# A hybrid encoder on one core: v of branch B ahead of the heads, silu gates of branch A behind pairs of heads, and sums of weights taken by VectorE

## The chip, the cores and the metric

The kernel runs on one core of a Trainium2 chip. The metric is the device time of one execution in microseconds, as the median of several runs; lower is better. Engines are named as in the profile: PE (TensorE, matmul), PEld (its weight loads), DVE (VectorE), ACT (ScalarE), POOL (GpSimd), SP (SyncE), and a q behind a name means the engine's own queue of DMA issues and waits.

## The reference

Two residual layers over 512 positions of width 1024. Each layer normalises its input, projects it once, and feeds three branches, whose gated outputs are merged and projected again.

```python
for l in range(DEPTH):
    h = rms_norm(x, norm_gain[l])
    proj = jnp.einsum('bld,dn->bln', h, w_in[l])
    (qa, fa_f, fa_b, ia, za, ub, vb, zb, qc, kc, vc, zc, g_a, g_b, g_c) = jnp.split(proj, split_at, axis=-1)
    ya = hgrn2_bidirectional(qa, fa_f, fa_b, ia, lower[l]).astype(x.dtype)
    ya = rms_norm(ya, hg_norm_gain[l]).reshape(B, L, HG_W) * jax.nn.silu(za)
    yb = spatial_gating(jax.nn.gelu(ub), jax.nn.gelu(vb), sg_ln_gain[l], sg_ln_bias[l],
                        w_spatial[l], b_spatial[l]) * jax.nn.silu(zb)
    ...
    yc = window_attention(qh, kh, vh, sink_logits[l]) * jax.nn.silu(zc)
    merged = (jax.nn.sigmoid(g_a) * jnp.einsum('blw,wd->bld', ya, w_branch_a[l])
              + jax.nn.sigmoid(g_b) * jnp.einsum('blw,wd->bld', yb, w_branch_b[l])
              + jax.nn.sigmoid(g_c) * jnp.einsum('blw,wd->bld', yc, w_branch_c[l]))
    x = x + jnp.einsum('bld,de->ble', merged, w_out[l])

def spatial_gating(u, v, ln_g, ln_b, w_s, b_s):
    vn = layer_norm(v, ln_g, ln_b).reshape(B, L // SG_CHUNK, SG_CHUNK, SG_GROUPS, SG_GW)
    mixed = jnp.einsum('gts,bnsgc->bntgc', w_s, vn) + b_s.T[None, None, :, :, None]
    return u * mixed.reshape(B, L, SG_W)
```

Branch A is a gated recurrence with four heads, run in both directions. Branch B mixes positions within chunks of 128 by a weight per group (w_s); v goes through a layer norm first. Branch C is attention in a window with eight query heads. The shift ln_b of the layer norm meets w_s in the mixing, so its part of the result is ln_b times the sum of each row of w_s: the kernel adds that to the bias b_s ahead of time.

## The kernel before, in words

Everything is float32. A product of activations and weights is done as three fast matmuls: both operands are split into a high part (a rounded copy by ACT, L267: wh of a weight) and a low part (a subtraction by DVE, L268: wl), and high x high, low x high and high x low are added up in PSUM (L470, L505, L517, L1172). The weights come in tiles of 128 x 1024 in the order of a list, weight_plan(). SP loads them (L239) in that order, some ahead of their use, and every tile is split once. Matmuls of plain float32 (the attention's values L831, the recurrence's L926 to L1029, the spatial mixing L1072, and the two products L1058) lie between them.

The weights of a layer come in this order: queries of branch C, its z gates and keys, the values of branch A (C_IA), then for each of the four heads of branch A the query, two forget gates and the z gate (C_QA, C_FF, C_FB, C_ZA), then v of branch B (C_VB), then the merge. Beside the blocks of weight matmuls run "sides": generators that do a piece of other work each time the main program calls advance(us). Such a generator yields the time that it has used, or None to wait for another turn. The attention is one side, begun before the heads; the gated recurrence of a pair of heads (gla) is added after each odd head; ln_v, which prepares the layer norm of v and the corrected bias, is added after v was projected; spatial mixing comes later. LAG and QLAG are numbers of turns that the attention lets pass between sending data through DRAM to transpose it and using it.

The build puts each engine's instructions into an order of its own, by when their inputs are ready; each engine then works in its order and stops at an instruction whose inputs are late. DMAs issued by SP or POOL stand in those engines' orders too.

Steps touched here, with lines of the profile: do_vb (L1045, gelu of v: ACT L1038 and L1040, DVE L1039 and L1041); ln_v (statistics L1053 and L1054, rstd L324 to L331, a matmul of ones with the weights ws L1058 whose result is each sum on all partitions, L1061 which adds the shift to the bias tile br, L1066 which normalises v); the z gates (L1095 and L1096); rope_row and rope_tables of the next layer (SP L336, SP L343, DVE L344), issued after head 1's block; the attention's scores (PE L781 and L782), their masked maxima (DVE L783), exponentials (ACT L795), scaling (DVE L806), transposes (DVE L813) and the way through DRAM (POOL L817, L818); and w_conv_to (L257), which adds two weights for a faster form of some products, the last of each layer on POOL.

Of the kernel before, what the change touches and what calls it, by code (L numbers as in the profile page):

```python
# [14 lines left out]
F32 = mybir.dt.float32  # L15
# [37 lines left out]
def weight_plan():  # L53

    plan = []

    def quarters(kind):

        for r, u in ((0, 0), (1, 0), (1, 1), (0, 1)):
            for i in range(2):  # L60
                plan.append(kind + (u, 2 * r + i))

    def nat(c):
        for i in range(4):
            plan.append(("n", c, i))

    nat(C_QC)
    for g in range(2):
        plan.append(("z", g))
    for i in range(2):  # L70
        plan.append(("k", C_KV, i))
    for g in range(2, 4):
        plan.append(("z", g))
    nat(C_IA)
    for h in range(H):
        for c in (C_QA, C_FF, C_FB, C_ZA):
            plan.append(("t", c + P * h))
    nat(C_VB)
    def merge(blocks):
        for n, j in enumerate(blocks):  # L80
            plan.append(("t", C_GC + P * j))
            if n % 2 == 0:
                plan.append(("b", 2, j, blocks[n + 1]))

    merge(MERGE[:6])

    quarters(("g", C_UB))
    for br, cg in ((0, C_GA), (1, C_GB)):
        quarters(("g", cg))
        for j in GATED:  # L90
            plan.append(("b", br, j, j + 1))
    merge(MERGE[6:])
    quarters(("o",))
    return plan
# [77 lines left out]
    return bass.AP(a.tensor, a.offset + off, [list(a.ap[0])] + [list(d) for d in dims])  # L172


def hybrid_kernel(tc, x, wpk, brow, gainb, pvec, wsp, trig, amask, imask, out):
    nc = tc.nc
    from contextlib import ExitStack

    with ExitStack() as es:
        cp = es.enter_context(tc.tile_pool(name="const", bufs=1))  # L180
        wp = es.enter_context(tc.tile_pool(name="wts", bufs=4))
        sb = es.enter_context(tc.tile_pool(name="work", bufs=2))
        pp = es.enter_context(tc.tile_pool(name="psum", bufs=3, space=PSUM))
        dp = es.enter_context(tc.tile_pool(name="spill", bufs=1, space=bass.MemoryType.DRAM))
        build(nc, tc, cp, wp, sb, pp, dp, x, wpk, brow, gainb, pvec, wsp, trig, amask, imask, out)


LAG, QLAG = 6, 9
N_M4, N_T2, N_PM, N_PS = 19, 7, 3, 5


def build(nc, tc, cp, wp, sb, pp, dp, x, wpk, brow, gainb, pvec, wsp, trig, amask, imask, out):
    V, S, G, E = nc.vector, nc.scalar, nc.gpsimd, nc.tensor


# [12 lines left out]
    def small(n):  # L208
        return sb.tile([P, n], F32, name=nm("sm"), tag="small", bufs=24)
# [4 lines left out]
    def ps_side(shape=(P, 512), dt=F32):  # L214
        return pp.tile(list(shape), dt, name=nm("ps"), tag="ps", bufs=N_PS)
# [29 lines left out]
    def raw(k):  # L245
        if k not in raws:
            w_load_to(k + 1)
        return raws[k]

    def w_conv_to(i, order=free, eng=V):  # L250
        while wstate["conv"] < min(i, len(OPERANDS)):
            n = wstate["conv"]
            k, add, form, _ = OPERANDS[n]
            r = raw(k)
            if form:
                raws[form[0]] = hold["t"][:, 2] if form[0][2] == 0 else m4()
                (G if form[0][1] % NW == NW - 8 else V).tensor_tensor(raws[form[0]], r, raw(form[1]), ALU.add)  # L257
            hi = wp.tile([P, 1024], F32R, name=nm("wh"), tag="wh", bufs=N_HI)
            lo = wp.tile([P, 1024], F32R, name=nm("wl"), tag="wl", bufs=N_LO)
            split(r, hi, lo, order, eng)  # L260
            if add is not None:
                G.dma_start(r, wpk[add], accum_op=ALU.add)
            his[n], los[n] = hi, lo
            wstate["conv"] += 1
# [326 lines left out]
    for l in range(L):  # L591
# [454 lines left out]
            gelu(po, vg[tb // 2][:, tb % 2, :])  # L1046

        def ln_v():
            mv = small(8)
            mv2 = mv.rearrange("p (n c) -> p n c", c=2)  # L1050
            for n in range(NT):
                st = small(6)
                V.bn_stats(st, vg[n // 2][:, n % 2, :])  # L1053
                V.bn_aggr(mv2[:, n, :], st)  # L1054
            r = rstd(mv2[:, :, 1], NT, 1.0)

            po = ps_side((P, 4, P))
            E.matmul(po, ones, ws, start=True, stop=True)  # L1058
            for g in range(4):
                b = br[:, g * P : (g + 1) * P]  # L1060
                V.scalar_tensor_tensor(b, po[:, g, :], lnb[:, g : g + 1], b, ALU.mult, ALU.add)  # L1061
            yield 2.5
            yield None
            for n in range(NT):
                v = vg[n // 2][:, n % 2, :]
                V.tensor_scalar(v, v, mv2[:, n, 0:1], r[:, n : n + 1], ALU.subtract, ALU.mult)  # L1066
                yield 0.7

        def spatial(g):
            po = ps_side((P, 4, P))  # L1070
# [6 lines left out]
            V.tensor_tensor(u, u, y.rearrange("p n t -> p (n t)"), ALU.mult)  # L1077
            yield 2.0


        glas = []
        lnv, spat = ln_v(), [spatial(g) for g in range(4)]
        for h in range(H):
            po = main_t()
            q = t2()
            S.copy(q, po)
            advance(2.6)
            ff, kd = m4((P, 2, T)), m4((P, 2, T))
            for d in range(2):
                po = main_t()  # L1090
                gates(po, d, h, ff, kd)
                advance(2.6)
            po = main_t()
            z = yA[h // 2][:, h % 2, :]
            S.activation(z, po, AF.Sigmoid)  # L1095
            V.scalar_tensor_tensor(z, po, hg[:, h : h + 1], z, ALU.mult, ALU.mult)  # L1096
            glas.append(gla(h, q, ff, kd, z))
            if h % 2 == 1:
                sides.append(together(glas[-2:]))
            advance(4.0)  # L1100
            if h == 1 and more:
                rr = rope_row(l + 1)
                tabs[0] = rope_tables(rr)
        nat_units(do_vb, 2.6)
        sides.append(lnv)

# [354 lines left out]
def host_arrays(inputs):  # L1463
    a = {k: np.asarray(v) for k, v in inputs.items()}
    ct = np.ascontiguousarray
    f = a["x"].dtype
    arrays = {}
    arrays["x"] = ct(a["x"].reshape(T, D))
    arrays["wpk"] = pack_weights(a["w_in"], a["w_branch_a"], a["w_branch_b"], a["w_branch_c"], a["w_out"])

    def swap(g):
        return np.concatenate([g[:, 32:], g[:, :32]], axis=1)

    qg, kg = a["q_norm_gain"], a["k_norm_gain"]
    arrays["brow"] = ct(
        np.concatenate(
            [
                a["b_spatial"].reshape(L, 512),
                qg,
                swap(qg),  # L1480
                kg,
                swap(kg),
                a["sink_logits"],
            ],
            axis=1,
        )
    )
    arrays["gainb"] = ct(a["norm_gain"])
    lbl = a["lb_logits"].reshape(L, 8, P).transpose(2, 0, 1).reshape(P, 16)
    hgt = a["hg_norm_gain"].transpose(2, 0, 1).reshape(P, 8)  # L1490
    lnt = [a[n].reshape(L, 4, P).transpose(2, 0, 1).reshape(P, 8) for n in ("sg_ln_gain", "sg_ln_bias")]
    arrays["pvec"] = ct(np.concatenate([lbl, hgt] + lnt, axis=1))
    arrays["wsp"] = ct(a["w_spatial"].transpose(0, 3, 1, 2))

    half = 32
    inv = (10000.0 ** (-np.arange(half, dtype=np.float64) / half)).astype(np.float32)
    ang = np.arange(T, dtype=np.float32)[:, None] * inv[None, :]
    c = np.cos(ang.astype(np.float64)).astype(np.float32)
    s = np.sin(ang.astype(np.float64)).astype(np.float32)
    cc = np.concatenate([c, c], axis=1).reshape(NT, P, 64).transpose(1, 0, 2)  # L1500
    sn = np.concatenate([-s, s], axis=1).reshape(NT, P, 64).transpose(1, 0, 2)
    arrays["trig"] = ct(np.stack([cc, sn], axis=1))
    qi, ki = np.arange(P)[:, None], np.arange(P)[None, :]
    arrays["amask"] = ct(
        np.concatenate(
            [np.where(ki >= qi, 0.0, MASKED), np.zeros((P, P)), np.where(ki <= qi, 0.0, MASKED)], axis=1
        ).astype(np.float32)
    )
    si, ti = (np.arange(P) % 32)[:, None], np.arange(32)[None, :]
    xr = si ^ ti  # L1510
    masks = [(xr >= m) & (xr < 2 * m) for m in (1, 2, 4, 8)]
    masks += [(xr < 16) & (np.arange(P)[:, None] // 32 == b) for b in range(4)]
    arrays["imask"] = ct(np.stack(masks, axis=1).astype(np.int32))
    assert arrays["x"].dtype == f
    return arrays


NAMES = ["x", "wpk", "brow", "gainb", "pvec", "wsp", "trig", "amask", "imask"]


# [16 lines left out]
```

## Time and profile before

| what | us |
|---|---|
| median of 3 runs | 1067.1 (1066.8 to 1068.72) |
| the profiled execution | 1067.53 |
| its span in the profile | 1065.8 |
| what lies around the span | 1.7 |
| granted TensorE clock | 1.00 |

In the profile, a row of instructions gives the engine, the line, the operation, the output tile and its inputs (in_ is a tensor in DRAM), how many there were and how long they took. Idle time before an instruction stands in brackets with what ended it. The rows of orders under the change hold no times: they are the instructions of one engine in the order in which it works through them.

### The profile page before, as it was taken

What the parts mean: (1) busy time and instruction counts of PE and PEld (TensorE: products, weight loads), DVE (VectorE), ACT (ScalarE), POOL (GpSimd) and SP (SyncE); (2) the same over time, 40 slices, a digit from 0 to 9 for tenths busy, and PEclk for the clock granted to TensorE, in tenths of its full rate; (3) what the DMA queues carried; (4) which work ended last, traced back from release to release, by engine and by line L of the source; (5) the groups of instructions that cost most, each with busy time, mean ns of one, the idle gap of its engine ahead of it and who ended that gap; (6) DMA issues with size and microseconds to landing.
All of it is one profiled execution on the core that took longest, in us unless ns stands there. A gap on an engine that the chain in (4) does not pass through costs nothing.

```text
span 1065.8 us, 19216 instructions
## 1 busy us (share of the span) xinstructions
PE 1054.4 (99%) x7720; PEld 904.8 (85%) x7720; DVE 822.4 (77%) x1525; ACT 536.1 (50%) x817; POOL 125.7 (12%) x178
## 2 busy tenths in 40 slices
PE   9999999999999999999999999999999999999998
PEld 8888777687889998988778887778778999999886
DVE  6885687779988776578897666887897877765885
ACT  5355865544336543545444367665433564445442
POOL 0220110100001110111102201100100011111020
PEclk9999999999999999999999999999999999999999
DMA  8663353932336865783947444543524378557755
GB/s 313 189 208 97 131 183 115 313 92 85 104 86 166 207 193 162 171 251 111 301 150 234 143 141 165 209 139 103 141 96 138 82 201 223 148 141 204 229 159 137
DMA packets 53768, 177.49 MB, mean 167 GB/s; under 512 B 6192, under 2 KB 10800, under 8 KB 53680
## 3 DMA queue, kind: packets, MB, share of 16 engines
q1 hardware_dynamic: 28656, 100.25, 28.1%
q0 software_dynamic: 23296, 71.84, 26.9%
q10 hardware_dynamic: 1728, 4.20, 1.0%
q8 instruction: 60, 0.98, 0.4%
q14 instruction: 28, 0.23, 0.1%
HBM read 154.23 MB, written 22.02 MB: 165 GB/s over the span
## 4 chain that ended last, share of the span: by engine, by line
PE 89%; DVE 6%; DMA 2%; ACT 1%; issue 1%; POOL 0%; SPq 0%; POOLq 0%; ACTq 0%; DVEq 0%
PE pm L517 39%; PE pm L1172 13%; PE ps L1172 13%; PE pm L470 11%; PE pm L505 2%; DMA wr<-in_wpk 2%; PE ps L831 2%; PE ps L926 1%; PE ps L1000 1%; DVE wl L268 1%; PE ps L781 1%; PE ps L782 1%; PE ps L317 1%; PE ps L1072 1%; PE ps L1011 1%
## 5 line engine op out<-in xcount | busy, mean ns | idle before, releaser
L267 ACT CAST wh<-wr 128x1024 fp32r<-128x1024 f32 x172 | 178.6, 1050 | 200.3 <-PE pm L517 113.4
L268 DVE TENSOR_TENSOR wl<-wr,wh 128x1024 fp32r<-128x1024 f32 x172 | 212.3, 1245 | 61.0 <-issue 22.5
L517 PE MATMUL pm<-hth,wh 128*128 128x512 f32 x448 | 177.1, 395 | 0.4 <-ACT wh L267 0.4
L517 PE MATMUL pm<-hth,wl 128*128 128x512 f32 x448 | 175.1, 391 | 0.3 <-DVE wl L268 0.3
L517 PE MATMUL pm<-htl,wh 128*128 128x512 f32 x448 | 175.1, 391 | 0.0
L517 PEld LDWEIGHTS pm<-hth,wh 128*128 128x128 f32 x448 | 84.1, 188 | 19.7 <-ACT wh L267 1.3
L517 PEld LDWEIGHTS pm<-hth,wl 128*128 128x128 f32 x448 | 84.1, 188 | 19.6 <-DVE wl L268 1.2
L517 PEld LDWEIGHTS pm<-htl,wh 128*128 128x128 f32 x448 | 84.2, 188 | 16.5
L517 PE MATMUL pm<-m,wh 128*128 128x512 f32 x256 | 90.9, 395 | 0.0
L470 PE MATMUL pm<-wh,hth 128*128 128x512 f32 x192 | 74.6, 398 | 0.7 <-ACT hth L267 0.5
L470 PE MATMUL pm<-wh,htl 128*128 128x512 f32 x192 | 73.6, 393 | 0.2 <-DVE htl L268 0.2
L470 PE MATMUL pm<-wl,hth 128*128 128x512 f32 x192 | 73.6, 393 | 0.0
L972 DVE TENSOR_TENSOR m<-m,f 128x512 f32<-128x512 f32 x96 | 62.8, 686 | 5.0 <-PE ps L957 3.3
L517 PEld LDWEIGHTS pm<-m,wh 128*128 128x128 f32 x256 | 47.5, 188 | 9.7 <-issue 0.5
L1172 PE MATMUL ps<-hth,wl 128*128 128x256 f32 x192 | 54.5, 284 | 0.6 <-DVE wl L268 0.6
L1172 PE MATMUL ps<-hth,wh 128*128 128x256 f32 x192 | 54.6, 284 | 0.0
L1172 PE MATMUL pm<-hth,wl 128*128 128x256 f32 x192 | 54.4, 283 | 0.0
L1172 PE MATMUL pm<-htl,wh 128*128 128x256 f32 x192 | 54.3, 283 | 0.0
L1172 PE MATMUL ps<-htl,wh 128*128 128x256 f32 x192 | 54.3, 283 | 0.0
L1172 PE MATMUL pm<-hth,wh 128*128 128x256 f32 x192 | 54.3, 283 | 0.0
L1172 PE MATMUL pm<-m,wh 128*128 128x256 f32 x288 | 52.8, 284 | 0.5 <-ACT m L1252 0.5
L268 DVE TENSOR_TENSOR wl<-hold,wh 128x1024 fp32r<-128x1024 f32 x32 | 39.1, 1222 | 18.0 <-PE pm L1172 17.2
(269 smaller groups left out, 2477.3 us busy)
## 6 DMA issues: line engine op xcount, KB each, us to landing
wr<-in_wpk SPq DMA_DIRECT2D x172, 512.0 KB, 4.5
hold<-in_wpk POOLq DMA_DIRECT2D x40, 512.0 KB, 5.6
pd<-m POOLq DMA_DIRECT2D x20, 512.0 KB, 3.5
m<-pd POOLq DMA_DIRECT2D x20, 512.0 KB, 5.5
wr<-in_wpk POOLq DMA_DIRECT2D x16, 512.0 KB, 6.0
m<-in_x SPq DMA_DIRECT2D x8, 512.0 KB, 7.5
m<-xd POOLq DMA_DIRECT2D x16, 256.0 KB, 7.0
m<-in_wpk POOLq DMA_DIRECT2D x8, 512.0 KB, 6.8
```

Source lines behind the costliest of these rows:

```text
L267: order(S.copy(hi_dst, src))
L268: order(eng.tensor_tensor(lo_dst, src, hi_dst.bitcast(F32), ALU.subtract))
L317: E.matmul(warm[:, :P], ident, ident, start=True, stop=True)
L470: E.matmul(po, a, b[:, o : o + 512], start=first and n == 0, stop=last and n == len(passes) - 1)
L505: E.matmul(po[:, k, :], a, b[:, o : o + 256], start=n == 0, stop=n == 23)
L517: E.matmul(po, s, m, start=n == 0, stop=n == 3 * nk - 1)
L781: E.matmul(sp[:, :nk], qt[qb][:, h, :], ktt[0][:, g, k0 * P : k1 * P], start=True, stop=False)
L782: E.matmul(sp[:, :nk], qt[qb][:, h, :], ktt[1][:, g, k0 * P : k1 * P], start=False, stop=True)
L831: E.matmul(po[64 * g : 64 * g + 64], vC[:, k0 + kb, 64 * g : 64 * g + 64], pt[:, :, 128 * g : 128 * g + 128], start=kb == 0, stop=kb == le ...
L926: E.matmul(cb[p0 : p0 + 32, slot, j // 4, :], kk(32 * j), qq(32 * j), start=True, stop=True, tile_position=(0, p0),)
L972: V.tensor_tensor(v, v, custom(ff, of, ([sd, 2], [2, ng], [0, m])), ALU.mult)
L1172: E.matmul(banks[g][:, r, :], a, b, start=not onto and (r, kt, n) == (0, 0, 0), stop=kt == 3 and n == 2, skip_group_check=onto is not None ...
```

## The change

The change has four parts.

- weight_plan: v of branch B (C_VB) comes ahead of the heads, and each pair of heads is followed by its two z gates (C_ZA) instead of each head by its own. The program follows: do_vb and ln_v's start come ahead of the loop over heads, and do_za(h), a new function with the old lines of the z gate, is called twice after each pair, behind the gated recurrence's start.
- ln_v: the matmul with ones goes. SP loads the transposed weights wsr (a new input, the same numbers in the order group, t, s), VectorE sums over s into ss (128 x 4), POOL stores these 512 numbers into DRAM and reads them back to all partitions into the same tile wsum, and the four steps that add to br read wsum from SBUF.
- LAG and QLAG go from 6 and 9 to 8 and 11.
- w_conv_to: all sums of two weights are VectorE's; before, POOL did the two adds of the last product of each layer.

```diff
@@ weight_plan
     nat(C_IA)
+    nat(C_VB)
     for h in range(H):
-        for c in (C_QA, C_FF, C_FB, C_ZA):
+        for c in (C_QA, C_FF, C_FB):
             plan.append(("t", c + P * h))
-    nat(C_VB)
+        if h % 2 == 1:
+            for g in (h - 1, h):
+                plan.append(("t", C_ZA + P * g))
...
-LAG, QLAG = 6, 9
+LAG, QLAG = 8, 11
...
-                (G if form[0][1] % NW == NW - 8 else V).tensor_tensor(raws[form[0]], r, raw(form[1]), ALU.add)
+                V.tensor_tensor(raws[form[0]], r, raw(form[1]), ALU.add)
...
         def ln_v():
+
+            wsum = t2((P, 4, P))
+            nc.sync.dma_start(wsum, wsr[l])
+            for _ in range(3):
+                yield None
+            ss = small(4)
+            V.tensor_reduce(ss, wsum, AX, ALU.add)
+            sd = dp.tile([4, P], F32, name=nm("sd"))
+            G.dma_start(sd.rearrange("g t -> t g"), ss)
+            G.dma_start(wsum.rearrange("p g t -> p (g t)"), sd.rearrange("g t -> (g t)").partition_broadcast(P))
+            yield 0.5
...
             r = rstd(mv2[:, :, 1], NT, 1.0)
-
-            po = ps_side((P, 4, P))
-            E.matmul(po, ones, ws, start=True, stop=True)
-            for g in range(4):
-                b = br[:, g * P : (g + 1) * P]
-                V.scalar_tensor_tensor(b, po[:, g, :], lnb[:, g : g + 1], b, ALU.mult, ALU.add)
             yield 2.5
             yield None
             for n in range(NT):
                 v = vg[n // 2][:, n % 2, :]
                 V.tensor_scalar(v, v, mv2[:, n, 0:1], r[:, n : n + 1], ALU.subtract, ALU.mult)
                 yield 0.7
+
+            for g in range(4):
+                b = br[:, g * P : (g + 1) * P]
+                V.scalar_tensor_tensor(b, wsum[:, g, :], lnb[:, g : g + 1], b, ALU.mult, ALU.add)
+            yield 0.5
...
+        def do_za(h):
+            po = main_t()
+            z = yA[h // 2][:, h % 2, :]
+            S.activation(z, po, AF.Sigmoid)
+            V.scalar_tensor_tensor(z, po, hg[:, h : h + 1], z, ALU.mult, ALU.mult)
+            advance(4.0)
...
         lnv, spat = ln_v(), [spatial(g) for g in range(4)]
+        nat_units(do_vb, 2.6)
+        sides.append(lnv)
         for h in range(H):
...
-            po = main_t()
-            z = yA[h // 2][:, h % 2, :]
-            S.activation(z, po, AF.Sigmoid)
-            V.scalar_tensor_tensor(z, po, hg[:, h : h + 1], z, ALU.mult, ALU.mult)
-            glas.append(gla(h, q, ff, kd, z))
+            glas.append(gla(h, q, ff, kd, yA[h // 2][:, h % 2, :]))
             if h % 2 == 1:
                 sides.append(together(glas[-2:]))
-            advance(4.0)
+                for g in (h - 1, h):
+                    do_za(g)
             if h == 1 and more:
                 rr = rope_row(l + 1)
                 tabs[0] = rope_tables(rr)
-        nat_units(do_vb, 2.6)
-        sides.append(lnv)
```

What this does to the orders is shown at three places of layer 0. Line numbers of the changed kernel are higher by 3 up to L1045 and by more behind that: L783, L806, L813 and L268 become L786, L809, L816 and L271; L1053 and L1061 become L1067 and L1079.

First SP's order around the load of rr, the rows of the next layer's rotary factors. Before (L239 loads a weight, L343 the tables):

```order
L239 DMA wr_1360<-in_wpk 128x1024
L239 DMA wr_1427<-in_wpk 128x1024
L239 DMA wr_1475<-in_wpk 128x1024
L336 DMA rr_1502<-in_brow 128x264
L343 DMA tabs_1504<-in_trig 128x512 x2
L239 DMA wr_1621<-in_wpk 128x1024
L239 DMA wr_1716<-in_wpk 128x1024
L239 DMA wr_1773<-in_wpk 128x1024
```

Of the change, the same place (L242 loads a weight, L339 rr):

```order
L242 DMA wr_1601<-in_wpk 128x1024
L242 DMA wr_1699<-in_wpk 128x1024
L242 DMA wr_1828<-in_wpk 128x1024
L339 DMA rr_1886<-in_brow 128x264
L346 DMA tabs_1888<-in_trig 128x512 x2
L242 DMA wr_1925<-in_wpk 128x1024
L242 DMA wr_2011<-in_wpk 128x1024
```

So rr's load stands five instructions later in SP's order: behind four more weights and the load of wsum, which is new (L1054, 13 weight loads ahead of rr). In VectorE's order the last read of the old rr (L794) stands ahead of the splits of wr_1601, wr_1699 and wr_1828; before, it stood behind the split of wr_1475, the last weight ahead of rr.

Second VectorE's order in the second block of the attention, from the scaling of its scores on. Before (wl_1424 is the low part of a weight; block 2's scores follow block 1's transposes):

```order
L806 TENSOR_SCALAR scores_1131<-scores_1131,sm_1126 128x3x128 x8
L1096 SCALAR_TENSOR_TENSOR m_187_1038<-pm_1213,pvc,m_187_1038 128x512
L813 STREAM_TRANSPOSE m_225_1254<-scores_1131 128x8x4x32
L813 STREAM_TRANSPOSE m_228_1272<-scores_1131 128x8x4x32
L813 STREAM_TRANSPOSE m_234_1297<-scores_1131 128x8x4x32
L844 TENSOR_TENSOR m_86_466<-ps_1317,m_86_466 128x2x128
L783 ISA scores_1327,sm_1324<-ps_1328,am,rows_574 128x3x128
```

Of the change (t_228 is wsum, br the bias tile; the rows behind these are one step of rstd between every two L786, eight L786 in all, and then the split of the first head's forget gate weight, L271 wl_1503):

```order
L816 STREAM_TRANSPOSE m_230_1293<-scores_1164 128x8x4x32
L816 STREAM_TRANSPOSE m_235_1313<-scores_1164 128x8x4x32
L1068 BN_AGGR sm_1350<-sm_1351 128x2
L1067 BN_STATS sm_1354<-m_196_1070 128x6
L1067 BN_STATS sm_1357<-m_203_1154 128x6
L816 STREAM_TRANSPOSE m_242_1345<-scores_1164 128x8x4x32
L1068 BN_AGGR sm_1350<-sm_1354 128x2
L1068 BN_AGGR sm_1350<-sm_1357 128x2
L1067 BN_STATS sm_1360<-m_203_1154 128x6
L1079 SCALAR_TENSOR_TENSOR br_1010<-t_228_1277,pvc,br_1010 128x128
L1068 BN_AGGR sm_1350<-sm_1360 128x2
L1079 SCALAR_TENSOR_TENSOR br_1010<-t_228_1277,pvc,br_1010 128x128
```

The statistics of v and the steps on br now lie between the transposes of one block and the scores of the next; the reduction (L1058) lies ahead of the eight scalings (L809).

Third TensorE's order at the first weights that follow (ps_1446 is the sixth of block 2's eight scores; there are five such places in PSUM, so it takes that of the first). Before, the ones matmul lay behind the heads:

```order
L517 MATMUL pm_2874<-hth_127,wh_2840 128x512
L517 MATMUL pm_2874<-htl_128,wh_2840 128x512
L517 MATMUL pm_2874<-hth_127,wl_2841 128x512
L1058 MATMUL ps_2973<-ws_1042,ones 128x512
L517 MATMUL pm_2979<-m_443_2670,wh_2939 128x512
```

Of the change, it is gone from there, and at the attention TensorE takes the high parts of three weights ahead before it needs wl_1503:

```order
L520 MATMUL pm_1465<-hth_127,wl_1433 128x512
L520 MATMUL pm_1522<-hth_127,wh_1502 128x512
L784 MATMUL ps_1446<-m_161_932,m_148_834 128x384
L785 MATMUL ps_1446<-m_162_933,m_148_834 128x384
L520 MATMUL pm_1522<-htl_128,wh_1502 128x512
L784 MATMUL ps_1450<-m_161_932,m_148_834 128x384
L785 MATMUL ps_1450<-m_162_933,m_148_834 128x384
L520 MATMUL pm_1567<-hth_127,wh_1552 128x512
L520 MATMUL pm_1567<-htl_128,wh_1552 128x512
L784 MATMUL ps_1454<-m_161_932,m_148_834 128x384
L785 MATMUL ps_1454<-m_162_933,m_148_834 128x384
L520 MATMUL pm_1629<-hth_127,wh_1597 128x512
```

So the sixth score follows 109 weight matmuls after the last score of block 1 (105 in layer 1), and pieces of three products follow before the first matmul with wl_1503.

More of the change, by code (lines that the diff above doesn't have):

```diff
@@ L172, in custom, with hybrid_kernel @@
     return bass.AP(a.tensor, a.offset + off, [list(a.ap[0])] + [list(d) for d in dims])
-def hybrid_kernel(tc, x, wpk, brow, gainb, pvec, wsp, trig, amask, imask, out):
+def hybrid_kernel(tc, x, wpk, brow, gainb, pvec, wsp, wsr, trig, amask, imask, out):
     nc = tc.nc
@@ L184, in hybrid_kernel, with build @@
         dp = es.enter_context(tc.tile_pool(name="spill", bufs=1, space=bass.MemoryType.DRAM))
-        build(nc, tc, cp, wp, sb, pp, dp, x, wpk, brow, gainb, pvec, wsp, trig, amask, imask, out)
-LAG, QLAG = 6, 9
+        build(nc, tc, cp, wp, sb, pp, dp, x, wpk, brow, gainb, pvec, wsp, wsr, trig, amask, imask, out)
+LAG, QLAG = 8, 11
 N_M4, N_T2, N_PM, N_PS = 19, 7, 3, 5
-def build(nc, tc, cp, wp, sb, pp, dp, x, wpk, brow, gainb, pvec, wsp, trig, amask, imask, out):
+def build(nc, tc, cp, wp, sb, pp, dp, x, wpk, brow, gainb, pvec, wsp, wsr, trig, amask, imask, out):
     V, S, G, E = nc.vector, nc.scalar, nc.gpsimd, nc.tensor
@@ L1493, in host_arrays @@
     arrays["wsp"] = ct(a["w_spatial"].transpose(0, 3, 1, 2))
+    arrays["wsr"] = ct(a["w_spatial"].transpose(0, 2, 1, 3))
     half = 32
@@ L1515, in host_arrays @@
     return arrays
-NAMES = ["x", "wpk", "brow", "gainb", "pvec", "wsp", "trig", "amask", "imask"]
+NAMES = ["x", "wpk", "brow", "gainb", "pvec", "wsp", "wsr", "trig", "amask", "imask"]
 def kernel(**inputs):
```

## The prediction

> **What bounds the kernel now.** I read the page's busy shares first, then what its chain consists of, then TensorE's waits, then the pace of its commonest piece.
>
> ```profile
> PE 1054.4 (99%) x7720; PEld 904.8 (85%) x7720; DVE 822.4 (77%) x1525; ACT 536.1 (50%) x817; POOL 125.7 (12%) x178
> ...
> PE 89%; DVE 6%; DMA 2%; ACT 1%; issue 1%; POOL 0%; SPq 0%; POOLq 0%; ACTq 0%; DVEq 0%
> ...
> 472.80 24.30 PE pm L517 x107
> ...
> PE ps L948 <- ACT t L915: 1.2, 1, 1.2
> PE ps L1172 <- DVE wl L268: 1.1, 2, 0.6
> PE pm L517 <- ACT wh L267: 0.4, 1, 0.4
> PE ps L948 <- DVE m L972: 0.4, 1, 0.4
> PE pm L517 <- DVE wl L268: 0.3, 1, 0.3
> ```
>
> TensorE is busy 99% of 1065.8 us and 89% of the chain that ended last; 107 weight matmuls in a row take 24.30 us, 0.227 us each. So a microsecond leaves this kernel in two ways only: TensorE does less, or it waits less. All of its idle time is 1065.8 - 1054.4 = 11.4 us, and the waits (us in total, times, longest) that touch lines near the change are the five quoted, 3.4 us together. VectorE with 77% is the next engine, and what matters is where it is full, not that share. The change moves no weight matmul out of the kernel, so its gain is small whatever happens: at most the two matmuls with ones and those waits.
>
> **What goes: the matmuls with ones.** Each layer loses one 128x512 matmul in plain fp32 (L1058).
>
> ```profile
> 274.60 1.02 PE L1058 MATMUL ps<-ws,ones 128*128 128x512 f32 x2
> 275.06 1.03 PE L517 MATMUL pm<-m,wh 128*128 128x512 f32 x2
> 275.93 0.40 PE L517 MATMUL pm<-m,wl 128*128 128x512 f32 x1
> ```
>
> The rows are start, duration and count, and one such matmul stands as two. From 274.60 to 275.93 are 1.33 us, in which two weight matmuls of 0.227 also run: 1.33 - 0.45 = 0.88 us for one, **1.75 us** for both layers, straight off the bound engine.
>
> **What goes: two places where TensorE waits.** In layer 0, rope_row's load of rr and its two tables stand in SP's queue ahead of four weights, and that load must first wait for the last attention block (L792).
>
> ```profile
> SPq L336 <- DVE sm L792: 40.1, 1, 40.1
> ...
> 182.31 0.33 SPq L336 DMA_DIRECT2D rr<-in_brow  x1
> ...
> 183.69 8.39 SPq L239 DMA_DIRECT2D wr<-in_wpk  x5
> ...
> 186.50 0.23 DVE L344 TENSOR_SCALAR rr<-rr 128x128 f32<-128x128 f32 x1 [1.87 <-DMA rr<-in_brow]
> ...
> 187.67 0.46 PE L948 MATMUL ps<-m,t 128*32 128x32 f32 x32 [0.39 <-DVE m L972]
> ...
> 189.31 1.05 ACT L267 CAST wh<-wr 128x1024 fp32r<-128x1024 f32 x1 [2.74 <-DMA wr<-in_wpk]
> 190.41 0.19 PEld L517 LDWEIGHTS pm<-hth,wh 128*128 128x128 f32 x1 [1.30 <-ACT wh L267]
> 190.41 0.50 PE L517 MATMUL pm<-hth,wh 128*128 128x512 f32 x1 [0.42 <-ACT wh L267]
> ```
>
> SP waits 40.1 us, weights go out from 183.69 on, ScalarE's cast waits 2.74 us for one of them, and VectorE, which works in order, stands 1.87 us before its own L972. TensorE pays 0.39 + 0.42 us and restarts slower (0.50 against 0.40 for the first matmul): about 1.0 us. In the SP rows shown with the change, v's four weights come ahead of rr. So when VectorE has read the old rr for the last time, the changed order has the splits of three loaded weights still ahead (wr_1601, wr_1699, wr_1828); before, every weight loaded ahead of rr was split by then. Three weights are 3 x 24 x 0.227 = 16.3 us for TensorE, and from SP's issue of rr to the next weight's arrival took 189.31 - 182.31 = 7.0 us: I count the 1.0 us as gone. If the attention's last block ends over 9 us later against the weights than the order has it, it comes back.
>
> In layer 1, ln_v's work falls among the gated recurrence of the last two heads:
>
> ```profile
> 760.00:790.00 30.00, 28.50 (x429) 21.08 (x418) 29.55 (x77) 14.61 (x20) 1.08 (x2) 1.00 0.28 90
> ...
> 787.24 0.46 PE L948 MATMUL ps<-m,t 128*32 128x32 f32 x32 [1.19 <-ACT t L915]
> ...
> 788.01 0.50 PE L517 MATMUL pm<-hth,wl 128*128 128x512 f32 x1 [0.31 <-DVE wl L268]
> ```
>
> In these 30 us VectorE is busy 29.55 (the third of the busy numbers, TensorE's is the first: 28.50), at a granted clock of 1.00. TensorE waits 1.19 + 0.31 us there, with two slower restarts 1.7 us. With v in front of the heads, ln_v (four L1053, four L1061, rstd and the normalising) is done some 100 us earlier: I count 1.7 us gone.
>
> The adds of L257 that POOL did go to VectorE:
>
> ```profile
> L257 POOL TENSOR_TENSOR m<-hold,wr x2: 2729/2900/3072, 513.8 to 1036.1; 128x1024 f32<-128x1024 f32 x2
> ...
> 489.10 2.41 POOL L257 TENSOR_TENSOR hold<-hold,wr 128x1024 f32<-128x1024 f32 x1 [13.27 <-DMA wr<-in_wpk]
> ...
> 489.19 3.40 DVE L268 TENSOR_TENSOR wl<-wr,wh 128x1024 fp32r<-128x1024 f32 x1 [0.41 <-PE pm L517]
> ...
> 139.60 1.22 DVE L268 TENSOR_TENSOR wl<-wr,wh 128x1024 fp32r<-128x1024 f32 x1
> 140.74 0.16 DVE L790 TENSOR_TENSOR sm<-sm,rr 128x8 f32<-128x8 f32 x1
> ```
>
> A split takes VectorE 1.22 us (the next starts after 1.14), but 3.40 while POOL's 2.41 us add runs beside it. So the hold adds cost VectorE nothing net: 1.22 more of its own, 2.2 less of that. The m adds (2.9 us on POOL) gate the splits behind the two 0.5 us waits of L1172 above; on VectorE they end some 1.7 us earlier, but the following reads there wait for other loads too, so I count 0.4 of these 1.1 us.
>
> Gone together: 1.75 + 1.0 + 1.7 + 0.4 = **4.85 us**.
>
> **What is added: ln_v beside the attention.** In the VectorE rows shown with the change, the reduction, four L1067, four L1079 and the small steps of rstd now stand inside the second attention block, ahead of the split wl of the first head's gate weight; before, that block was followed by four splits with little between. These are the prices (start and duration):
>
> ```profile
> 126.84 3.19 DVE L806 TENSOR_SCALAR scores<-scores,sm 128x384 f32<-128x384 f32 x8
> ...
> 130.60 3.48 DVE L813 STREAM_TRANSPOSE m<-scores 128x1024 f32<-128x1024 f32 x3
> ...
> 134.85 0.61 DVE L783 CUSTOM_DVE_ANT_0 scores<-ps,am,rows 128x384 f32<-128x384 f32 x1
> ...
> 135.39 0.61 DVE L783 CUSTOM_DVE_ANT_0 scores<-ps,am,rows 128x384 f32<-128x384 f32 x1
> ...
> 269.54 1.25 DVE L1053 BATCH_NORM_STATS2 sm<-m 128x6 f32<-128x512 f32 x2
> ...
> 276.46 0.34 DVE L1061 SCALAR_TENSOR_TENSOR br<-ps,pvc,br 128x128 f32<-128x128 f32 x1
> ...
> L1019 DVE TENSOR_REDUCE sm<-t x8: 676/679/687, 245.7 to 835.7; 128x4 f32<-128x512 f32 x8
> ...
> L795 ACT ACTIVATE scores<-scores,sm x64: 492/554/619, 100.8 to 718.7; 128x256 f32<-128x256 f32 x32, 128x384 f32<-128x384 f32 x32
> L889 ACT ACT_TABLE_LOAD x8 | 10.3, 1283 | 0.1
> ```
>
> The chain from the last score matmul of block 1 to the place in PSUM that the sixth score of block 2 needs: VectorE reads the score, does two splits and the gelu step, 3.9 us; ScalarE does eight exponentials (0.6) with a sigmoid between them and three table loads (1.28), 9.4 us; VectorE then does eight scalings 3.1, three transposes 3.4, the reduction 0.6, four L1053 2.4, four L1061 1.0, small steps 1.1 and one L783 0.6: 12.2 us. That is 25.5 us, and 26.1 with 0.6 for hand-offs. TensorE has, by its order, 109 weight matmuls and ten score matmuls to do meanwhile in layer 0, 105 and ten in layer 1: at 0.227 and 0.17 (an estimate, three quarters of 0.227) 26.4 and 25.5 us. The two sides meet within what such a count can tell, about 1 us. I take stalls of 0.3 us in layer 0 and 1.0 in layer 1, and 0.7 for the splits right behind, which have no slack left: **2.0 us** added, with ends of 0 and 5. Before, the splits there had those 5 us of ln_v (0.6 + 2.4 + 1.0 + small steps) not ahead of them. Two more table loads (2 x 1.28) lie on an engine that is busy 50%; I cost them at nothing, as they count in the 9.4. Of VectorE's other additions, four adds of 1.22 are dealt with above.
>
> **What is added: the way through DRAM.** The reduction is stored as 512 elements of 4 bytes, read back to all partitions, and only then may L1079 run. Columns here: count, KB each, median us from issue to landing.
>
> ```profile
> vd<-t POOLq DMA_DIRECT2D x4, 128.0 KB, 4.0
> xd<-t POOLq DMA_DIRECT2D x4, 128.0 KB, 2.2
> htl<-h POOLq DMA_DIRECT2D x2, 512.0 KB, 13.0
> br<-in_brow SPq DMA_DIRECT2D x2, 256.0 KB, 4.5
> ```
>
> The read back has the form of br, 256 KB to 128 partitions: 4.5 us. No row has a store of single elements; the nearest is a small store to DRAM, 2.2 to 4.0 us, the far end the slowest transfer of that queue, 13.0. I take 4.0, as it is the same queue and small. Round trip 8.5 us (6.7 to 17.5). From the reduction to the first L1079, VectorE has 3.1 + 3.4 + 2.4 + 0.2 = 9.1 us of other work. So it costs 0 as forecast, with 0.6 us to spare. If it comes later, VectorE stops at L1079, behind which the eight L783 and the split wait, and TensorE stops for them in both layers. The Trainium skill, "DMA: Bandwidth & Descriptors", section "Specifications", says that transfers below 512 bytes are done by read-modify-write, and its section "Anatomy of one DMA — SWDGE (gpsimd) path" that a fixed 2.0 us, mostly the receipt of the write, can get surprisingly long when DRAM is written: it speaks against this step, and no run here has such a store. By its 2.0 us twice and 0.6 for the bytes the round trip would be an estimated 4.6 us, and the sum the same.
>
> **The sum.** The profiled run took 1067.53 us, 0.43 above the median of the runs shown. 1067.53 - 4.85 + 2.0 = 1064.7 for that run, so 1064.25 against the median 1067.1: **1064.2 us**, 0.27% less.
>
> **Rivals.** *All gain, no new stall* (the 2.0 are 0): 1067.1 - 4.85 = 1062.2; for it speaks that the order gives TensorE 26.4 us against 26.1, against it that layer 1 has less. *The waits only move*: VectorE's full stretch goes from 760-790 to the attention, stalls are 3 to 5 us, and of the 4.85 about what the ones matmuls give or nothing is left: 1065.3 to 1067.2. For it speaks that VectorE's total doesn't fall. *Slower*: the round trip exceeds 9.1 us. From there each microsecond costs two (both layers). With 10.5 us it gives 1064.2 + 2.8 = 1067.0; it ends slower than 1069.2 from 11.6 us on (2 x 2.5); the far end of 17.5 would give 1064.2 + 16.8 = 1081. For it speaks that single elements are more pieces than any store here has, against it the small stores of 2.2 and 4.0. *The change does not do what it says*: the sums may be exact and off TensorE, but if the gate weights run late behind each pair, one split more waits, 0.3 us, within the forecast.
>
> **How the numbers follow.** Chances: forecast 0.45 (1062.8 to 1065.6), all gain 0.13, waits move 0.25, slow round trip 0.17, of which 0.08 over 1069.2. 0.2% is 2.1 us, about what a measurement can tell: faster is below 1065.0, slower above 1069.2. Faster: two thirds of the forecast (0.32), all of the first rival, 0.05 of the others: 0.50. Slower: 0.10 with 0.02 for what I don't see. Same: 0.40. The range leaves out half of the first rival and the slow tail: 1061.5 to 1068.8.
>
> **What would show it.** TensorE's busy time falls by 1.8; no L1058 on TensorE; no wait of ScalarE's cast at the load of rr; no wait of TensorE in the last heads of layer 1. The new stalls, if any, are TensorE waits for wl or a score's place in PSUM at 125 to 160 us and 665 to 700. VectorE idle before L1079 by the DMA of wsum means the slow rival; the length of that idle time is the price in its layer. The forecast is wrong if TensorE's idle time, now 11.4 us, does not fall.

## The result, and the profile after

The changed kernel takes 1074.1 us (median of 4 runs, 1073.22 to 1074.87), the kernel before in the same comparison 1067.68 (1066.8 to 1068.72). The ratio is 1.0057, with a 95% interval of 1.0045 to 1.007: slower by 0.57%, where 1064.2 and 0.27% faster were forecast. The range was 1061.5 to 1068.8, and 1074.1 lies above it.

The page's first part:

```profile
span 1072.3 us, 19220 instructions
...
PE 1053.5 (98%) x7716; PEld 904.1 (84%) x7716; DVE 819.2 (76%) x1531; ACT 538.1 (50%) x819; POOL 118.5 (11%) x178
```

TensorE idles for 18.8 us in place of 11.4. Its longest wait (us in total, times, longest):

```profile
PE ps L784 <- DVE sm L786: 8.8, 2, 4.7
```

The waits at L948 and L517 quoted from before are not in the list any more, and neither is one at the next layer's rr. In their stead stands a new one, 8.8 us in two times, of the attention's scores for VectorE. What VectorE does then is in its timeline of layer 0 (start, duration, in brackets the idle time before it and what ended it):

```profile
133.80 0.63 DVE L1058 TENSOR_REDUCE sm<-t 128x4 f32<-128x512 f32 x1
134.35 3.29 DVE L809 TENSOR_SCALAR scores<-scores,sm 128x384 f32<-128x384 f32 x8
...
142.94 0.65 DVE L1067 BATCH_NORM_STATS2 sm<-m 128x6 f32<-128x512 f32 x1
148.60 0.35 DVE L1079 SCALAR_TENSOR_TENSOR br<-t,pvc,br 128x128 f32<-128x128 f32 x1 [5.00 <-DMA t<-sd]
...
149.93 0.61 DVE L786 CUSTOM_DVE_ANT_0 scores<-ps,am,rows 128x384 f32<-128x384 f32 x1
```

The reduction ends at 134.4, the other work at 143.6, 9.2 us later; then VectorE stands still for 5.00 us until the sums are back. TensorE needs the place in PSUM that L786 at 149.93 reads, and waits in its turn. Its rows in layer 0 and layer 1:

```profile
150.61 0.44 PE L784 MATMUL ps<-m,m 128*128 128x384 f32 x1 [4.03 <-DVE sm L786]
...
679.13 0.69 PE L784 MATMUL ps<-m,m 128*128 128x384 f32 x1 [4.73 <-DVE sm L786]
```

The two transfers in the view of DMA issues (count, KB each, median us to landing) say why VectorE waits:

```profile
t<-sd POOLq DMA_DIRECT2D x2, 256.0 KB, 4.8
...
sd<-sm POOLq DMA_DIRECT2D x2, 2.0 KB, 8.7
```

The store of 2 KB takes 8.7 us, longer than the read back of 256 KB. Those 2 KB are 512 pieces of 4 bytes; a piece is a run of bytes that lies together on both sides of the transfer. In layer 0 POOL issues the store at 134.7 and it lands at 143.4. The DMA engines' own work for it is short, as two windows show (the share of the DMA engines that is busy is the second number from the end):

```profile
135.70:136.50 0.80, 0.80 (x5) 0.68 (x4) 0.80 (x4) 0.80 (x2) 0.00 (x0) 1.00 0.23 3
136.50:141.00 4.50, 4.50 (x23) 3.90 (x23) 4.50 (x8) 4.37 (x7) 0.00 (x0) 1.00 0.00 0
```

By the trace's records of DMA packets all 2048 bytes of the store are through by 136.43, 1.7 us after the issue. The other 7.0 us lie between its last packet and the landing, and the trace doesn't show what happens in them.

And the wait costs more than its length, as the windows after it show (TensorE's busy time first; the clock that TensorE was granted, as a share of full speed, is the third number from the end):

```profile
150.00:151.00 1.00, 0.39 (x2) 0.40 (x3) 1.00 (x5) 0.00 (x0) 0.62 (x1) 1.00 0.37 152
151.00:152.00 1.00, 1.00 (x5) 0.86 (x4) 1.00 (x7) 0.00 (x0) 1.00 (x3) 0.63 0.34 41
152.00:153.00 1.00, 1.00 (x4) 0.81 (x4) 1.00 (x7) 0.00 (x0) 0.44 (x1) 0.50 0.99 111
153.00:154.00 1.00, 1.00 (x4) 0.52 (x2) 1.00 (x5) 0.00 (x0) 0.00 (x0) 0.50 0.77 201
154.00:155.00 1.00, 1.00 (x5) 0.44 (x6) 1.00 (x7) 0.00 (x0) 0.00 (x0) 0.66 1.02 410
155.00:156.00 1.00, 1.00 (x6) 0.14 (x2) 1.00 (x2) 0.00 (x0) 0.00 (x0) 1.00 1.02 414
```

TensorE is busy all the time from 151 to 155, but at 0.63, 0.50, 0.50 and 0.66 of its clock: 0.37 + 0.50 + 0.50 + 0.34 = 1.7 us of work are lost. In layer 1 the wait is 4.73 us, and the clock falls at 676.9, during the wait, and is still low when TensorE goes on at 679.13:

```profile
679.00:680.00 1.00, 0.86 (x3) 0.87 (x4) 1.00 (x7) 0.00 (x0) 1.00 (x2) 0.50 0.06 25
...
683.00:684.00 1.00, 1.00 (x6) 0.38 (x4) 1.00 (x4) 0.00 (x0) 0.00 (x0) 0.63 1.04 410
684.00:685.00 1.00, 1.00 (x7) 0.19 (x4) 1.00 (x3) 0.00 (x0) 0.00 (x0) 1.00 0.93 377
```

0.86 x 0.5, three times 0.5 and 0.37 are 2.3 us more. Both layers together: 8.8 of waiting and 4.0 of low clock, 12.8 us. Without them the span would be some 1059.5 us, 6 less than before.

### The profile page after: what moved, and what is told of

Same layout as the page of the kernel before. It is cut to its first block, busy times and chain, and to the rows that moved or that the text cites. A ratio compares the mean times of both kernels' runs of the same rounds, so it can differ in the third digit from the quotient of the medians.

```text
span 1072.3 us, 19220 instructions
## 1 busy us (share of the span) xinstructions
PE 1053.5 (98%) x7716; PEld 904.1 (84%) x7716; DVE 819.2 (76%) x1531; ACT 538.1 (50%) x819; POOL 118.5 (11%) x178
## 4 chain that ended last, share of the span: by engine, by line
PE 79%; issue 12%; DVE 4%; DMA 3%; ACT 1%; POOL 1%; SPq 0%; POOLq 0%; ACTq 0%; DVEq 0%
PE pm L520 37%; PE pm L1189 13%; PE ps L1189 13%; PE pm L473 4%; PE pm L508 2%; DMA wr<-in_wpk 2%; PE ps L834 2%; PE ps L929 1%; DVE wl L271 1%; PE ps L1003 1%; DMA t<-sd 1%; PE ps L1014 1%; PE ps L1085 1%; PE ps L951 1%; PE ps L1018 0%
## 5 line engine op out<-in xcount | busy, mean ns | idle before, releaser
L271 DVE TENSOR_TENSOR wl<-wr,wh 128x1024 fp32r<-128x1024 f32 x172 | 207.0, 1217 | 66.5 <-issue 23.0
L1189 PE MATMUL ps<-m,wh 128*128 128x256 f32 x288 | 52.6, 283 | 0.0
```

The lines of the kernel that those rows point to most:

```text
L271: order(eng.tensor_tensor(lo_dst, src, hi_dst.bitcast(F32), ALU.subtract))
L1189: E.matmul(banks[g][:, r, :], a, b, start=not onto and (r, kt, n) == (0, 0, 0), stop=kt == 3 and n == 2, skip_group_check=onto is not None ...
```

## The experiments

Theory 1 was that the way through DRAM costs all of it; theory 2, that VectorE is overfull where ln_v lies beside the attention, whatever it waits for. Times are medians; ratios are against runs of the kernel before on the same chip, which lay at 1066.9 (e1 to e4), 1067.3 (e5 to e8) and 1067.05 (e9, e10). The changed kernel's 1074.1 was measured against 1067.68, so runs of different groups are best compared by their ratios.

**e1: the sums earlier.**

```diff
+        sd = dp.tile([4, P], F32, name=nm("sd"))
+        def sums_of_weights():
+            w0 = t2((P, 4, P))
+            nc.sync.dma_start(w0, wsr[l])
+            for _ in range(1):
+                yield None
+            ss = small(4)
+            V.tensor_reduce(ss, w0, AX, ALU.add)
+            G.dma_start(sd.rearrange("g t -> t g"), ss)
+            yield 0.5
+        sides.append(sums_of_weights())
         nat_units(do_ia, 2.6)
...
         def ln_v():
             wsum = t2((P, 4, P))
-            nc.sync.dma_start(wsum, wsr[l])
-            for _ in range(3):
-                yield None
-            ss = small(4)
-            V.tensor_reduce(ss, wsum, AX, ALU.add)
-            sd = dp.tile([4, P], F32, name=nm("sd"))
-            G.dma_start(sd.rearrange("g t -> t g"), ss)
             G.dma_start(wsum.rearrange("p g t -> p (g t)"), sd.rearrange("g t -> (g t)").partition_broadcast(P))
-            yield 0.5
+            for _ in range(3):
+                yield None
```

> The changed kernel with the reduction and its store moved ahead of branch A's values; the read back stays with the start of ln_v, into a tile of its own. Theory 1 (the way through DRAM): store 8.7 us and read back 4.8 us make VectorE wait 5.0 us in each layer, TensorE 4.0 and 4.7 us for it, and the clock of 0.5 that follows costs about 1.6 and 2.1 us more. All 12.4 us go: 1074.1 - 12.4 = 1061.7, no wait before the steps on br, clock 1.00. Theory 2 (VectorE is overfull where ln_v lies beside the attention, whatever it waits for): most of the wait stays as back to back work, 1069 or more.

1077.23 us, ratio 1.0098 (1.0082 to 1.0114): slower still, and neither theory's number. A row of VectorE, a row of TensorE and the windows behind them:

```profile
97.02 1.14 DVE L1086 SCALAR_TENSOR_TENSOR br<-t,pvc,br 128x128 f32<-128x128 f32 x4 [13.64 <-DMA t<-sd]
...
98.88 0.39 PE L785 MATMUL ps<-m,m 128*128 128x256 f32 x1 [2.61 <-DVE m L755]
...
100.00:101.00 1.00, 1.00 (x4) 0.76 (x4) 1.00 (x2) 0.00 (x0) 0.00 (x0) 0.56 0.04 4
101.00:102.00 1.00, 1.00 (x4) 0.80 (x3) 1.00 (x3) 0.00 (x0) 0.00 (x0) 0.50 0.88 225
```

The build moved the steps on br along with the sums, ahead of the attention, to where it took the read back to be done, with hardly any work between: the wait is 13.64 us there. So starting earlier does not help where the consumer is moved too, and e1 does not separate the theories. It does show a low clock again, here 1.2 us after TensorE has gone on from a wait of 2.61 us. TensorE's list has more waits than that one:

```profile
PE ps L785 <- DVE m L755: 4.8, 2, 2.6
PE pm L520 <- ACT m L906: 3.3, 1, 3.3
PE ps L784 <- DVE sm L786: 2.6, 2, 1.9
```

A low clock comes with both waits of the first row and behind the 3.3 us of the second, each time for 3.4 us; none comes with the 1.9 us of the third row, where it stays at 1.00.

**e2: the matmul with ones back, at the new place.** The reduction, both transfers and the new steps on br go; the two removed lines with E.matmul(po, ones, ws) and the four old steps on br return.

> The changed kernel with the sums by the matmul with ones again, at the new place of ln_v; no reduction, no DRAM. Theory 1: as e1 plus the two matmuls of 0.88 us: 1063.4. Theory 2: 1069 or more, since statistics, br and rstd stay beside the attention.

1066.77 us (1064.63 to 1070.57), ratio 1.0004 (0.9992 to 1.0015): as fast as before within the interval. TensorE's longest wait there:

```profile
PE ps L784 <- DVE sm L786: 2.7, 2, 1.4
```

The two waits of 4.0 and 4.7 are down to 1.4 at most without a transfer, so the long ones are the transfer's. The time is between the theories' numbers. But e2 has an order of its own: the steps on br stand ahead of the second block's scalings, and the 1.4 us lie in the third block, where e3 below has no wait.

```profile
124.87 1.13 DVE L1064 SCALAR_TENSOR_TENSOR br<-ps,pvc,br 128x128 f32<-128x128 f32 x4
...
172.32 0.36 PE L784 MATMUL ps<-m,m 128*128 128x256 f32 x1 [1.38 <-DVE sm L786]
```

So e2 does not show that VectorE is overfull at the changed kernel's order; why the 2.7 us come there stays open.

**e3: pieces of 16 bytes.**

```diff
-            sd = dp.tile([4, P], F32, name=nm("sd"))
-            G.dma_start(sd.rearrange("g t -> t g"), ss)
+            sd = dp.tile([P, 4], F32, name=nm("sd"))
+            G.dma_start(sd, ss)
...
-            G.dma_start(wsum.rearrange("p g t -> p (g t)"), sd.rearrange("g t -> (g t)").partition_broadcast(P))
+            G.dma_start(wsum.rearrange("p g t -> p (g t)"), sd.rearrange("t g -> (t g)").partition_broadcast(P))
...
-                V.scalar_tensor_tensor(b, wsum[:, g, :], lnb[:, g : g + 1], b, ALU.mult, ALU.add)
+                V.scalar_tensor_tensor(b, wsum.rearrange("p g t -> p (g t)").rearrange("p (t g) -> p g t", g=4)[:, g, :], lnb[:, g : g + 1], b, ALU.mult, ALU.add)
```

> The changed kernel, but the 512 sums are stored as they lie, 128 pieces of 16 bytes in place of 512 of 4, and the steps on br read the tile with a stride of four elements. If the 8.7 us of the store go by the number of pieces above about 2.2 us: 2.2 + 6.5/4 = 3.8 us, round trip about 9.2, no wait left to speak of, 1061 to 1063. If every store of small pieces takes as long: 1074.

1062.42 us, ratio 0.9957 (0.9942 to 0.9972): **faster than both kernels**. By the traces, TensorE, VectorE and ScalarE go through the same instructions in the same order as in the changed kernel, and so they do in e5 and e6 below. The transfers in the view of DMA issues:

```profile
t<-sd POOLq DMA_DIRECT2D x2, 256.0 KB, 3.7
...
sd<-sm POOLq DMA_DIRECT2D x2, 2.0 KB, 1.7
```

And the page's first part:

```profile
span 1059.1 us, 19220 instructions
...
PE 1050.8 (99%) x7716; PEld 902.9 (85%) x7716; DVE 819.5 (77%) x1531; ACT 537.9 (51%) x819; POOL 118.4 (11%) x178
```

The same 2 KB are stored in 1.7 us, VectorE does not wait for them, TensorE idles for 8.3 us, and with one layout some 11 us of the changed kernel are gone (1.0057 against 0.9957). Theory 1 holds. The time between the store's last packet and its landing is 0.4 us here, where it was 7.0. And e3 lies 4.35 us below e2 on the same chip: e2's waits of 2.7 and its two matmuls of 1.75 add up to 4.45.

**e4: the sums through DRAM only**, in the kernel before, with its order of blocks (the diff's ln_v and nothing else).

> The kernel before with only the sums of weights by VectorE and through DRAM, v behind the heads as before, turns 6 and 9. VectorE has about 10.8 us of work between reduction and the steps on br there. Theory 1: it waits up to 3.3 us per layer, and TensorE part of that: 1065.3 (two matmuls less) to 1071. Theory 2: no wait, 1065.3.

1066.12 us, ratio 0.9993 (0.9984 to 1.0003). The store takes 8.6 us here too, and VectorE waits in both layers:

```profile
DVE br L1076 <- DMA t<-sd: 4.8, 2, 2.6
```

At most 2.6 us, since more work lies between (10.9 us, from 271.9 to 282.8); TensorE has 1.4 us of new waits at L1015, behind it. Two matmuls are saved and the wait of layer 1 at ln_v goes, but only 0.8 us is left of that, which is within the noise.

**e5: pieces of 8 bytes**: as e3, with sd as two halves of [P, 2], 256 pieces.

> The changed kernel with the sums stored as 256 pieces of 8 bytes; VectorE's order is that of the changed kernel. If the store goes by the number of pieces (8.7 us for 512, 1.7 for 128: 18 ns each), it takes 1.7 + 128 x 0.018 = 4.0 us, and with a read back of 3.7 to 4.8 and two issues of 0.6 the round trip is about 9, so VectorE waits 0 to 1 us and the time is that of e3, 1062 to 1064. If only pieces of 4 bytes are slow: 1.7 us and 1062. If all under 16 bytes are: 8.7 us and 1074.

1061.91 us, ratio 0.9948 (0.9933 to 0.9963), the fastest of all with e9. The store:

```profile
sd<-sm POOLq DMA_DIRECT2D x2, 2.0 KB, 3.4
```

1.7 us for 128 pieces, 3.4 for 256, 8.7 for 512: the time goes up with the pieces, and by more per piece from 256 to 512 (5.3 us) than from 128 to 256 (1.7). Nearly all of it comes behind the last packet: 0.4, 1.9 and 7.0 us to the landing, while the packets are through 1.3, 1.5 and 1.7 us after the issue. These runs change the number of pieces, their size and their spacing in DRAM together, so which of them sets the time stays open. VectorE does not wait for the sums here.

**e6: the store by ScalarE's queue**: nc.scalar.dma_start in place of G.dma_start for the 512 pieces.

> The changed kernel with the store of 512 pieces of 4 bytes issued by ScalarE in place of POOL. If the 8.7 us belong to POOL's queue: 2 to 3 us, no wait, 1062. If they belong to the pieces: about 8.7 us again, 1074.

1071.31 us, ratio 1.0039 (1.0028 to 1.0051). It takes as long there:

```profile
sd<-sm ACTq DMA_DIRECT2D x2, 2.0 KB, 8.2
```

So it is the pieces, not POOL's queue; the packets are through after 1.3 us here, and the landing comes 6.9 us behind them. VectorE waits 4.0 us per layer in place of 5.0, and by the ratios the kernel is some 1.9 us faster than the changed one, though the two intervals overlap.

**e7: e3 with LAG and QLAG at 6 and 9.**

> e3 (pieces of 16 bytes) with LAG and QLAG at 6 and 9 as before the change. If the longer turns are part of the gain: slower than e3's 1062.4 by 0.5 to 3 us, with waits of TensorE for the attention's data (L784, L834). If not: 1062.4 within 1.

1075.34 us, ratio 1.0078 (1.0063 to 1.0093), worse than expected and in another place than expected: not the attention's data are late but the sums again. The windows around the store, which runs at 139.9 us, with the DMA share as the second number from the end:

```profile
135.00:140.00 5.00, 5.00 (x25) 4.36 (x24) 5.00 (x15) 2.40 (x4) 2.42 (x4) 1.00 0.89 279
140.00:145.00 5.00, 5.00 (x22) 3.76 (x22) 5.00 (x17) 0.29 (x1) 0.42 (x1) 1.00 0.81 313
```

The store among its DMA issues:

```profile
sd<-sm POOLq DMA_DIRECT2D x2, 2.0 KB, 6.6
```

The changed kernel's own row for the first of these windows:

```profile
135.00:140.00 5.00, 5.00 (x25) 4.29 (x24) 5.00 (x10) 4.97 (x7) 0.48 (x1) 1.00 0.04 0
```

With fewer turns the reduction comes behind the transposes, and its store behind their six transfers of 512 KB; the DMA engines are busy 0.81 to 0.89 and even 128 pieces take 6.6 us. That time lies elsewhere than in the changed kernel: the first packet starts 3.4 us after the issue (e3: 1.1), the last one ends after 5.1 and 6.7 us, and the landing follows 0.7 us later. VectorE waits 5.4 us at most. In the changed kernel the engines were idle (0.04) when its store took 8.7, so there it was not the load.

**e8: pieces of 16 bytes only**, in the kernel before (e4 with e3's layout).

> The kernel before with only the sums by VectorE and through DRAM in pieces of 16 bytes; order of blocks and turns as before. Round trip 1.7 + 3.7 + 1.1 = 6.5 us, less than the 10.8 us of work there, so no wait at the steps on br (e4: 2.6 and 2.2 us) and the stalls of 1.0 and 0.7 us at L1015 gone: 1066.9 - 1.75 = 1065.2. If the order of the blocks gives the rest of e3's gain, it lies 2.8 us above e3; if the sums are all of the gain, it is as fast as e3, 1062.4.

1063.3 us, ratio 0.9967 (0.9953 to 0.998). No wait for the sums, though the store takes 3.7 us and not 1.7; the DMA engines are busy 0.6 while it runs. In TensorE's list the waits of layer 0 at the next layer's rr remain, and those of layer 1 at ln_v are gone:

```profile
sd<-sm POOLq DMA_DIRECT2D x2, 2.0 KB, 3.7
...
PE ps L948 <- DVE m L972: 0.6, 1, 0.6
...
PE pm L517 <- ACT wh L267: 0.4, 1, 0.4
```

So most of the gain, 4.0 us of the 5.4 that e5 has on the same chip, needs no new order of blocks.

**e9: e5 with POOL's adds as before.**

> e5 (pieces of 8 bytes, 1061.9) with the two adds of each layer's last product on POOL again, as before the change. The prediction gave moving them to VectorE 0.4 us for the splits behind the adds and nothing for the rest: 1062.3. If POOL's adds beside VectorE cost more than that (the split of 3.4 us): up to 1064. If VectorE is better off without them: below 1061.5.

1061.85 us (5 runs), ratio 0.9953 (0.994 to 0.9966), against 1061.91 of e5 (ratio 0.9948): who does the adds makes no difference that can be measured.

**e10: the new order of blocks only.**

> The kernel before with the new order of blocks only (v ahead of the heads, z gates behind pairs); the matmul with ones, turns 6 and 9 and POOL's adds as before. The prediction's steps: 1.0 and 1.7 us of waits go, and 2.0 come beside the attention: 1066.9 - 0.7 = 1066.2. If the waits at the attention are those of e2 (1.5 us in each layer) and no others: 1066.9 - 2.7 + 3.0 = 1067.2. If the turns of 6 and 9 need other work between: slower than 1069.

1077.28 us (1073.08 to 1084.04), ratio 1.0104 (1.0076 to 1.0131). TensorE's longest waits:

```profile
PE ps L1180 <- DVE wl L271: 2.7, 4, 1.4
PE ps L834 <- DMA m<-pd: 2.2, 2, 1.6
```

With turns of 6 and 9 the values of the attention come before their data are back from DRAM. The low clock comes too, once, from 676.7 on, behind one of these waits:

```profile
676.28 1.58 PE L834 MATMUL ps<-m,t 128*64 128x512 f32 x2 [1.61 <-DMA m<-pd]
...
677.00:678.00 1.00, 1.00 (x3) 0.21 (x2) 1.00 (x2) 1.00 (x4) 0.00 (x0) 0.50 1.04 279
```

The order of blocks alone is a loss. e2 has the same order of blocks and the same matmul with ones, and differs by turns of 8 and 11 and by the adds, which made no difference in e9: 1.0004 there against 1.0104 here, so the order needs the longer turns. The waits listed do not add up to the 10 us, and the runs scatter over 11, so the rest of this loss stays open.

## Why the prediction was wrong

- **The matmuls with ones**, 1.75 us less: they are gone (7716 records in place of 7720), and the difference of e2 and e3 fits the size. TensorE's busy time doesn't show it: 1050.5 us in e2 with them, 1050.8 in e3 without.
- **The wait at rr**, 1.0 us: right; e3 and e5 don't have it, while e8, with the old order, does.
- **The wait at ln_v in layer 1**, 1.7 us: gone as forecast, but moving v was not needed for it. In e8 v stays where it was, and the wait goes with the matmul of ones; why it goes there is not shown.
- **The adds of L257**, 0.4 us: nothing measurable (e9).
- **The new stalls beside the attention**, 2.0 us: too much. In e5 TensorE waits 0.7 us there, for ScalarE and not for VectorE. The count of 26.1 us against 26.4 and 25.5 was close, as e3 shows with the read of the first score and the matmul that needs its place, in layer 0 and in layer 1: 0.7 us to spare in the one, and just in time in the other.

```profile
145.05 0.62 DVE L786 CUSTOM_DVE_ANT_0 scores<-ps,am,rows 128x384 f32<-128x384 f32 x1
146.40 0.33 PE L784 MATMUL ps<-m,m 128*128 128x384 f32 x1
...
666.90 0.60 DVE L786 CUSTOM_DVE_ANT_0 scores<-ps,am,rows 128x384 f32<-128x384 f32 x1
667.57 0.44 PE L784 MATMUL ps<-m,m 128*128 128x384 f32 x1
```

- **The turns**, LAG and QLAG: the prediction has no term for them and gives no reason. It is not why it missed, but they carry much of the change: with 6 and 9 the kernel of e3 goes from 0.9957 to 1.0078 (e7), and that of e2 from 1.0004 to 1.0104 (e10).
- **The way through DRAM**, the step that failed: the prediction put the store of 512 single elements at 4.0 us, as the nearest small stores of 2.2 and 4.0, and so the round trip at 8.5, inside the 9.1 us of other work. The other work measured 9.2, the read back 4.8 against 4.5; the store took 8.7, and the round trip 14.2 (134.4 to 148.6). The store was mis-sized by 4.7 us, and the bounds (2.2 to 13.0) did hold it. The rival was the right one with its place, but at 0.17 it was given too little, and about half of it lay outside the range: 0.6 us to spare is no cover for a price that no row shows.
- **The price of the wait** was too low as well: the rival had two us for each us past the cover, which is 10.0 for 5.0. Measured are 8.8 of waiting and 4.0 of low clock, which the prediction had no term for. That 1064.2 + 10.0 comes near 1074.1 is luck: the kernel without the wait is at 1061.9 (e5), not 1064.2, and the wait costs some 12.

The case that all is gained and no new stall comes (1062.2) is what e3 and e5 measure (1062.4 and 1061.9). So the 4.85 us of gains stood as a total, though the 0.4 of the adds isn't seen and the 2.0 of new stalls didn't come.

## What to carry to other kernels

Price a small store by its pieces and not by its bytes alone: the same 2 KB took 1.7 to 8.7 us here. Lay the data out so that each partition writes one piece, and read it with a stride behind. A round trip through DRAM whose length no row of the trace shows should have a cover of nearly twice the guess (8.5 us were guessed here and 14.2 measured), or its consumer should stand behind the work that the bound engine waits for; e1 shows that starting earlier doesn't help if the consumer moves along. On a kernel that keeps TensorE at 99%, count a stall of 4 us or more at about one and a half times its length (8.8 us of waiting cost 12.8 here), since the clock falls with it.

## What the runs showed of the hardware

- 2 KB to DRAM took 8.7 us as 512 pieces of 4 bytes (8.2 from ScalarE's queue), 3.4 as 256 of 8 and 1.7 as 128 of 16, in the changed kernel's order, where the DMA engines were nearly idle. Their packets were through 1.3 to 1.7 us after the issue; the rest, 7.0, 1.9 and 0.4 us, lay between the last packet and the landing. The 128 pieces took 3.7 us (e8) with the DMA engines 0.6 busy and 6.6 us (e7) with them over 0.7 busy, and there the packets came late. The Trainium skill, "DMA: Bandwidth & Descriptors", section "Anatomy of one DMA — SWDGE (gpsimd) path", has a fixed 2.0 us, mostly the receipt of the write, and says that many descriptors can be emitted before their cost shows. The 1.7 us is near the fixed time, the 8.7 us is not, and the measurement decides. The second fits POOL's issuing instruction, which took only 0.2 us more for 512 pieces than for 128 (0.76 and 0.56).
- The granted clock fell to 0.50 around TensorE's waits of 4.03 and 4.73 us, for 3.4 us in layer 0 (from 151.3) and 6.8 in layer 1 (from 676.9). In e1 it fell for 3.4 us after a wait of 2.61 us as well, and only after TensorE had gone on (on again at 98.88, low from about 100.1 by the 0.56 of the window from 100); behind a wait of 1.9 us it stayed at 1.00. In e10 it fell after one of 1.61 us, so the length of the wait alone doesn't tell. The Trainium skill, "TensorE: Matmul & The Clock Gate", section "Part 1: The HAM clock gate (the "warmup" mystery)", states a half clock after an idle stretch of at least one free-running window of about 3.4 us, and the full clock after a busy one. The length of the low stretches agrees, one window or two, while the waits of 2.61 and 1.61 us are shorter than that window and had the same effect.
